# Transposing layer 1's queries in 128-column squares instead of per-head blocks of 96

## The chip, the cores and the metric

The kernel runs on one core of one Trainium2 chip. The metric is device time in microseconds. The kernel before has a median of 1709.44 us over three runs (1705.8 to 1714.31).

A core has five engines, each with its own in-order queue: TensorE (PE; its weight loads are shown apart as PEld), VectorE (DVE), ScalarE (ACT), GpSimd (POOL) and SyncE (SP), which here issues nearly all DMA transfers.

## The reference

Two transformer-like layers run over 1024 latent tokens and 256 context tokens of width 1024. Layer 0 is grouped-query attention, layer 1 multi-head latent attention with 16 heads. The part that matters here is how layer 1 makes its queries: a compressed projection of 384 columns is normalised, expanded to 16 heads x 96, normalised per head, and its last 32 of 96 entries are rotated. Scores are products of 96-long vectors.

```
def q_heads(q_a, n):
    q = (rms_norm(q_a, p["q_a_norm"]) @ p["w_q_b"]).reshape(B, n, MLA_HEADS, MLA_NOPE + MLA_ROPE)
    q = rms_norm(q, p["q_norm"])
    return jnp.split(q, [MLA_NOPE], axis=-1)
...
s = (jnp.einsum('bqhd,bkhd->bhqk', q_nope, k_nope)
     + jnp.einsum('bqhr,bkr->bhqk', q_rope, k_rope)).astype(jnp.float32) * ((MLA_NOPE + MLA_ROPE) ** -0.5)
p = jax.nn.softmax(s, axis=-1).astype(v.dtype)
return jnp.einsum('bhqk,bkhd->bqhd', p, v)
```

All of it is float32. The kernel keeps each matrix operand as two parts: a rounded high part and the remainder (low part). It forms a product from three matrix products, high x high, high x low and low x high (`mm3`, lines 93 to 95).

## The kernel before, in words

Layer 1 starts near 890 us. First keys and values are made, then (from about 990 us) the queries, then the attention over 16 heads (from about 1157 us), then the output projection (to the end).

The queries are made for 8 tiles of 128 tokens. For a tile, `q_compress` multiplies the modulated input by 384 columns and normalises (qan, line 1631). `q_latent` transposes that in three 128x128 blocks (line 1638) and splits it in a high part qah and a low part qal, which are also stored in memory (qad). `q_expand` multiplies them by 768 columns of the expansion weights, as two groups of 384 columns, and normalises and rotates; a group is four heads of 96 and lies as [128 tokens, 384 columns] in a tile t. `q_store` transposes each group into the layout that attention reads (columns on partitions, tokens along the row), splits it with `split` (ACT's copy th at line 86, DVE's subtraction tl at line 87) and stores both parts in device memory, in q1h and q1l, shaped [16 heads, 96, 1024 tokens].

The 768 columns are half of the 16 heads, so the 8 tiles are gone through twice. The first pass makes qah and qal; the second fetches them from qad. Each pass has 8 x 2 groups, so `q_store` handles 32 groups in all. Gate products (`gate_slice`, three matrix products per step, stored to sgd with gth) are mixed in, to give PE work in between. Also mixed in are weight loads (`load_weight`): a raw tile wraw is loaded, ACT rounds it to wa (line 157), and POOL or DVE makes the remainder wb (line 136).

Buffers around `q_store`: the transposes write into one of four PSUM tiles tp, which is free again when the subtraction tl has read it. The split writes into two staging tiles th and two tl, which are free when their store has landed.

Attention loads, for each head, the queries in halves of 512 tokens: QH (64 rows of q1h), QR (the 32 rotary rows), QL and QS (the same of q1l), with the keys KH and KL from k1h and k1l. First come maxima of the scores (mx, lines 393 and 403), then the scores (st, line 501), exponentials (p), and products with the values (av, line 555). KS is a key tile that is loaded when the last gate product has left its place (line 1529).

Outside a few parts that are written in a fixed order, the order of the instructions on each engine is set when the program is built, by a scheduler that goes by dependencies and by its own costs of instructions. A changed shape can therefore move neighbours, transfers on SP's queue among them.

Of the kernel before, what the change touches and what calls it, by code (L numbers as in the profile page):

```python
# [19 lines left out]
P = 128  # L20
# [11 lines left out]
def raw(ap):  # L32
    return ap.bitcast(F32)
# [3 lines left out]
def hybrid_kernel(ctx: ExitStack, tc: tile.TileContext, ins: dict, out: bass.AP):  # L37
    nc = tc.nc
    pe, act, dve, pool, sp = nc.tensor, nc.scalar, nc.vector, nc.gpsimd, nc.sync
# [16 lines left out]
    ident = const.tile([P, P], F32, name="ident")  # L56
# [13 lines left out]
    q1h = dram.tile([16, 96, NL], F32, name="q1h")  # L70
    q1l = dram.tile([16, 96, NL], F32, name="q1l")
# [13 lines left out]
    def split(hi, lo, src):  # L85
        act.copy(hi, src)  # L86
        dve.tensor_sub(lo, src, raw(hi))  # L87
# [975 lines left out]
    rows = {}  # L1063
# [530 lines left out]
    for p_ in range(8):  # L1594
        for par in range(2):
            h = 2 * p_ + par
# [6 lines left out]
    with ExitStack() as st:  # L1603
# [78 lines left out]
        def q_store(tt, c, held):  # L1682
            cs = slice(tt * P, (tt + 1) * P)
            for q4 in range(2):
                h0 = 8 * c + 4 * q4
                tp = ps_tp.tile([P, 512], F32, name="tp", tag="tp")
                for j in range(4):
                    pe.transpose(tp[:96, j * P:(j + 1) * P], held[q4][:, j * 96:(j + 1) * 96], ident)
                th = sg2.tile([P, 4, P], F32R, name="th", tag="th")
                tl = sg2.tile([P, 4, P], F32R, name="tl", tag="tl")  # L1690
                split(th[:96], tl[:96], tp[:96, :].rearrange("p (a n) -> p a n", n=P))
                sp.dma_start(q1h[h0:h0 + 4, :, cs].rearrange("a p n -> p a n"), raw(th[:96]))
                sp.dma_start(q1l[h0:h0 + 4, :, cs].rearrange("a p n -> p a n"), raw(tl[:96]))

        wqb = [load_weight(ins["l1_w_q_b"], 3, 0, 768,
                           slot=[wqp.tile([P, 2304], F32R, name=n) for n in ("wqa1", "wqb1")])]
# [6 lines left out]
        def store(c):  # L1703
            return lambda tt, held: q_store(tt, c, held)
# [95 lines left out]
```

## Time and profile before

| | |
|---|---|
| Median of three runs | 1709.44 us (1705.8 to 1714.31) |
| Profiled execution, own time | 1707.59 us |
| Its span | 1705.8 us |
| PE busy | 1667.9 us, 98% |
| DVE busy | 1046.6 us, 61% |
| POOL busy | 961.4 us, 56% |
| ACT busy | 645.1 us, 38% |
| Transposes of `q_store` | 128, first at 1030.1, last at 1134.8 us |
| Stores to q1h and to q1l | 32 and 32, 192 KB each |

The profile is of one execution. Times in its rows are microseconds from the start of the span; a row of the timeline gives start, duration, engine, line, operation, tiles (out<-in), shapes and count, and in brackets how long the engine had been idle and what ended that. A matrix product's recorded duration overlaps with its neighbours, so the cost of one in a run is the distance between starts. A row of waits says which instruction waited for which, for how long in total, how many times, and the longest. In rows with a bar the figures behind it are busy time in total, mean ns of one, and idle time before.

### The profile page before, as it was taken

To read this page: it belongs to the slowest core of one execution; us is meant where nothing else is said; L and a number is where in the kernel's file an instruction comes from. 1 tells how busy PE (TensorE), PEld (TensorE's weight loads), DVE (VectorE), ACT (ScalarE), POOL (GpSimd) and SP (SyncE) were. 2 spreads that over 40 slices of the span, in tenths; PEclk is the share of its full clock that TensorE was granted. 3 is DMA by queue.
4 is the path that set the end of the run, shared out by engine and by line. 5 is a ranking of instruction groups with operands and counts; after the bars stand their busy time and mean duration, and the time that the engine had idled before them with its cause. 6 is when DMAs were issued, how large, how long until landed. Compare 5 with 4: busy or idle time off the path is not lost. (4 is left out here: it accounts for less than half of the span.)

```text
span 1705.8 us, 27449 instructions
## 1 busy us (share of the span) xinstructions
PE 1667.9 (98%) x10244; PEld 1196.9 (70%) x10244; DVE 1046.6 (61%) x1807; ACT 645.1 (38%) x943; POOL 961.4 (56%) x646
## 2 busy tenths in 40 slices
PE   8999999999999999999989999999999999999998
PEld 5776778775555555557878898986767667667587
DVE  3765552357778777625675657754677777777231
ACT  4642221124445544432244533340434444344310
POOL 2763431218789988743245544350668787787511
PEclk9999999999999999999999999999999999999999
DMA  9557754521242422146433766766565655653452
GB/s 315 169 150 241 253 176 142 152 81 45 63 121 61 112 63 63 38 137 204 139 94 117 233 189 182 207 192 164 135 137 134 134 122 121 146 124 91 125 160 74
DMA packets 219821, 238.97 MB, mean 140 GB/s; under 512 B 23016, under 2 KB 159192, under 8 KB 219688
## 3 DMA queue, kind: packets, MB, share of 16 engines
q1 hardware_dynamic: 219264, 237.11, 49.5%
q8 instruction: 81, 1.33, 0.3%
q14 instruction: 52, 0.43, 0.1%
q10 hardware_dynamic: 424, 0.11, 0.0%
HBM read 163.37 MB, written 73.63 MB: 139 GB/s over the span
## 5 line engine op out<-in xcount | busy, mean ns | idle before, releaser
L395 DVE TENSOR_REDUCE m<-mx 128x1 f32<-128x512 f32 x512 | 336.2, 687 | 176.3 <-PE mx L393 170.5
L508 ACT ACTIVATE p<-st 128x1024 f32<-128x1024 f32 x328 | 336.0, 1027 | 169.8 <-PE st L501 134.8
L542 POOL TENSOR_TENSOR acp<-acp,p 128x1024 f32<-128x1024 f32 x128 | 305.8, 2389 | 7.8
L555 PE MATMUL av<-p,v 128*64 128x512 f32 x1312 | 289.9, 595 | 0.0
L555 PEld LDWEIGHTS av<-p,v 128*64 128x64 f32 x1312 | 90.9, 137 | 180.6 <-issue 177.9
L542 POOL TENSOR_TENSOR acp<-p 128x1024 f32<-128x1024 f32 x34 | 81.4, 2396 | 148.0 <-ACT p L508 147.9
L542 POOL TENSOR_TENSOR acp<-acp,acd 128x1024 f32<-128x1024 f32 x60 | 142.2, 2370 | 22.3 <-DVE acd L528 19.1
L528 DVE TENSOR_REDUCE acd<-p 128x512 f32<-128x1024 f32 x124 | 144.7, 1220 | 7.9 <-ACT p L508 7.8
L136 POOL TENSOR_TENSOR wb<-wraw,wa 128x512 fp32r<-128x512 f32 (+3 forms) x73 | 95.4, 1326 | 81.2 <-ACT wa L157 81.2
L93 PE MATMUL mm<-wa,hh 128*128 128x512 f32 (+2 forms) x336 | 127.4, 379 | 1.1 <-ACT hh L890 1.1
L501 PE MATMUL st<-QH,KH 64*128 64x512 f32 x320 | 122.2, 404 | 1.0 <-DVE gth L303 1.0
L95 PE MATMUL mm<-wa,hl 128*128 128x512 f32 (+2 forms) x336 | 121.5, 362 | 1.6 <-DVE hl L893 1.6
L94 PE MATMUL mm<-wb,hh 128*128 128x512 f32 (+2 forms) x336 | 121.2, 361 | 0.0
L501 PE MATMUL st<-QH,KL 64*128 64x512 f32 x320 | 119.0, 392 | 0.0
L501 PE MATMUL st<-QL,KH 64*128 64x512 f32 x320 | 118.3, 390 | 0.0
L576 ACT COPY os<-av 128x512 f32<-128x512 f32 x36 | 21.1, 587 | 255.9 <-PE av L555 205.9
L93 PE MATMUL y<-wa,oh 128*128 128x512 f32 (+1 forms) x296 | 114.1, 386 | 1.4 <-DVE yt L750 1.4
L95 PE MATMUL y<-wa,ol 128*128 128x512 f32 (+1 forms) x296 | 113.5, 384 | 0.0
L94 PE MATMUL y<-wb,oh 128*128 128x512 f32 (+1 forms) x296 | 113.5, 383 | 0.0
L404 DVE TENSOR_REDUCE m<-mx 128x2 f32<-128x512 f32 x144 | 95.4, 688 | 24.0 <-PE mx L403 18.9
L393 PE MATMUL mx<-KH,QH 64*128 64x512 f32 x256 | 102.7, 405 | 0.5 <-DVE m L404 0.3
L93 PE MATMUL mm<-hh,wa 128*128 128x512 f32 x256 | 102.0, 399 | 0.5 <-ACT th L86 0.5
(240 smaller groups left out, 4023.1 us busy)
## 6 DMA issues: line engine op xcount, KB each, us to landing
mraw<-in_l_w_mod SPq DMA_DIRECT2D x64, 256.0 KB
wraw<-in_l_w_in SPq DMA_DIRECT2D x28, 512.0 KB
KH<-k1h SPq DMA_DIRECT2D x32, 320.0 KB
KL<-k1l SPq DMA_DIRECT2D x32, 320.0 KB
rb<-rrow SPq DMA_DIRECT2D x72, 128.0 KB
mraw<-in_l_w_mod SPq DMA_DIRECT2D x16, 512.0 KB
sgd<-gth SPq DMA_DIRECT2D x32, 256.0 KB
wraw<-in_l_w_out SPq DMA_DIRECT2D x16, 512.0 KB
```

Of the source, the lines that this page charges most:

```text
L93: pe.matmul(ps, lhsT=lh(k), rhs=rh(k), start=first and i == 0, stop=False)
L94: pe.matmul(ps, lhsT=lh(k), rhs=rl(k), start=False, stop=False)
L95: pe.matmul(ps, lhsT=ll(k), rhs=rh(k), start=False, stop=last and i == len(ks) - 1)
L136: eng.tensor_sub(lo, a, b)
L393: pe.matmul(held["m"][:, cs], lhsT=q[:, t * P:(t + 1) * P], rhs=k[:, ks], start=j == 0, stop=j == len(pairs) - 1)
L395: dve.reduce_max(s["m"][:, i, n:n + 1], held["m"], axis=AX.X)
L404: dve.reduce_max(s["m"][:, 2 * i:2 * i + 2, 2 if u["kind"] == "lat" else 0], m.rearrange("p (a b) -> p a b", a=2), axis=AX.X)
L501: pe.matmul(ps[:, n * 512:(n + 1) * 512], lhsT=lh, rhs=rh, start=j == 0, stop=j == last)
L508: act.activation(p, ps, AF.Exp, scale=self.ops["scale"])
L528: dve.reduce_sum(t[:, ns], p2.rearrange("p a n -> p n a")[:, ns, :], axis=AX.X)
L542: pool.tensor_add(t, a, b)
L555: pe.matmul(s["av"][64 * n:64 * n + 64, :], lhsT=s["v"][:, kt, u["vc"]:u["vc"] + 64], rhs=p[:, n * 512:(n + 1) * 512], start=kt == kts[0], ...
```

## The change

`q_store` no longer transposes a group head by head. Before, four transposes took 96 columns each and wrote 96 partitions of the tile tp, four blocks of 128 tokens side by side: [96, 4 x 128]. Now three transposes take 128 columns each and write all 128 partitions: [128, 3 x 128]. The 384 columns of a group are the same, and so are the bytes. Row r of the three blocks put under each other is column r of the group, and because q1h is contiguous, (head, 96) can be read as 1536 rows, of which a group covers three blocks of 128. So the copy, the subtraction and the two stores now have the shape 128 x 3 x 128 where they had 96 x 4 x 128. What lies in memory is the same, and the loads of attention are not touched.

```
-                h0 = 8 * c + 4 * q4
+                rows = slice(3 * (2 * c + q4), 3 * (2 * c + q4) + 3)
                 tp = ps_tp.tile([P, 512], F32, name="tp", tag="tp")
-                for j in range(4):
-                    pe.transpose(tp[:96, j * P:(j + 1) * P], held[q4][:, j * 96:(j + 1) * 96], ident)
+                for j in range(3):
+                    pe.transpose(tp[:, j * P:(j + 1) * P], held[q4][:, j * P:(j + 1) * P], ident)
                 th = sg2.tile([P, 4, P], F32R, name="th", tag="th")
                 tl = sg2.tile([P, 4, P], F32R, name="tl", tag="tl")
-                split(th[:96], tl[:96], tp[:96, :].rearrange("p (a n) -> p a n", n=P))
-                sp.dma_start(q1h[h0:h0 + 4, :, cs].rearrange("a p n -> p a n"), raw(th[:96]))
-                sp.dma_start(q1l[h0:h0 + 4, :, cs].rearrange("a p n -> p a n"), raw(tl[:96]))
+                split(th[:, :3], tl[:, :3], tp[:, :384].rearrange("p (a n) -> p a n", n=P))
+                for dst, src in ((q1h, th), (q1l, tl)):
+                    sp.dma_start(dst.rearrange("h d n -> (h d) n").rearrange("(a p) n -> a p n", p=P)[rows, :, cs].rearrange("a p n -> p a n"),
+                                 raw(src[:, :3]))
```

The scheduler's order moves in three places that the prediction speaks of. On DVE, early in the query stage, this is the order before (t is a group's tile; wb the remainder of a weight piece, L136; tl the subtraction of `q_store`, L87):

```order
L1670 TENSOR_TENSOR t_10657<-mm,cwq 128x384
L1675 TENSOR_TENSOR qt_10659<-mm,swq 128x8x8 x2
L136 TENSOR_TENSOR wb<-wraw,wa 128x768
L1678 TENSOR_TENSOR t_10657<-t_10657,q_rs 128x384
L1665 TENSOR_REDUCE qss<-sq 128x4
L1670 TENSOR_TENSOR t_10682<-mm,cwq 128x384
L117 TENSOR_SCALAR q_ms<-qss 128x4
L1675 TENSOR_TENSOR qt_10684<-mm,swq 128x8x8 x2
L87 TENSOR_TENSOR tl<-tp,th 96x512
```

And now:

```order
L1670 TENSOR_TENSOR t_10655<-mm,cwq 128x384
L1675 TENSOR_TENSOR qt_10657<-mm,swq 128x8x8 x2
L1665 TENSOR_REDUCE qss<-sq 128x4
L1678 TENSOR_TENSOR t_10655<-t_10655,q_rs 128x384
L117 TENSOR_SCALAR q_ms<-qss 128x4
L1670 TENSOR_TENSOR t_10680<-mm,cwq 128x384
L1675 TENSOR_TENSOR qt_10682<-mm,swq 128x8x8 x2
L87 TENSOR_TENSOR tl<-tp,th 128x384
```

The weight piece wb no longer stands ahead of tl; it follows about 25 rows behind tl, and the reduction qss has moved up by one.

On SP, at the seam between the gate products and the first scores, this is the order before (QS from crow is a row of the maxima, sgd a gate store, v a load of values):

```order
L1541 DMA KH<-k1h 64x1280
L427 DMA QS<-crow 1x4x128 x2
L1529 DMA KS<-kr1h 32x1280
L304 DMA sgd_96<-gth 128x512
L1529 DMA KS<-kr1h 32x1280
L358 DMA v<-vd_94 128x10x128
L1542 DMA QH<-q1h 64x512
L1544 DMA QR<-q1h 32x512 x2
```

And now:

```order
L1541 DMA KH<-k1h 64x1280
L427 DMA QS<-crow 1x4x128 x2
L1542 DMA QH<-q1h 64x512
L1529 DMA KS<-kr1h 32x1280
L304 DMA sgd_96<-gth 128x512
L1529 DMA KS<-kr1h 32x1280
L358 DMA v<-vd_94 128x10x128
L1544 DMA QR<-q1h 32x512 x2
```

One load of QH has moved from behind the two KS loads to ahead of them.

On PE, at the end of the first pass, these are the transposes of two token tiles before (t is a group's tile, qah and qal the operands of the expansion):

```order
L1688 MATMUL tp<-ident,t_10739 96x128 x4
L1688 MATMUL tp<-ident,t_10764 96x128 x4
L1688 MATMUL tp<-ident,t_10811 96x128 x4
L1688 MATMUL tp<-ident,t_10836 96x128 x4
L93 MATMUL mm<-wa,qah 128x384
```

And now:

```order
L1688 MATMUL tp<-ident,t_10735 128x128 x3
L1688 MATMUL tp<-ident,t_10760 128x128 x3
L1688 MATMUL tp<-ident,t_10805 128x128 x3
L1688 MATMUL tp<-ident,t_10830 128x128 x3
L93 MATMUL mm<-wa,qah 128x384
```

Each group has three transposes where it had four, at the same place between the products.

## The prediction

> **What bounds the kernel now.** I read the page's busy times first, then the stages.
>
> ```profile
> span 1705.8 us, 27449 instructions
> PE 1667.9 (98%) x10244; PEld 1196.9 (70%) x10244; DVE 1046.6 (61%) x1807; ACT 645.1 (38%) x943; POOL 961.4 (56%) x646
> ```
>
> TensorE (PE) is busy for all but 37.9 of 1705.8 us, so what matters of an edit is what it takes out of PE's queue and what it does to PE's few waits. The busy table by stretch shows where the queries are made (1028 to 1146), the seam (1146 to 1210) and layer 1's attention behind it; columns are PE, weight loads, DVE, ACT, POOL, clock, DMA share, GB/s.
>
> ```profile
> 1028.00:1146.00 118.00, 114.56 (x628) 102.50 (x628) 85.10 (x209) 44.34 (x88) 54.69 (x65) 1.00 0.73 197
> 1146.00:1160.00 14.00, 13.79 (x58) 10.12 (x56) 3.31 (x6) 2.24 (x4) 2.54 (x2) 1.00 0.98 250
> 1160.00:1210.00 50.00, 47.10 (x245) 33.80 (x246) 26.03 (x41) 9.15 (x11) 8.68 (x5) 1.00 0.62 171
> 1210.00:1600.00 390.00, 389.95 (x2921) 261.20 (x2919) 279.31 (x403) 167.02 (x173) 294.90 (x142) 1.00 0.52 121
> ```
>
> In attention PE idles 0.05 of 390 us: nothing there can swallow or return a shift, so whatever the query stage saves or loses arrives at the end of the program in full. In the query stage PE idles 118.00 - 114.56 = 3.4 us. The waits of PE's instructions (and one of ACT's) between 990 and 1240 name the parts: us in total, times, longest.
>
> ```profile
> PE tp L1688 <- DVE tl L87: 2.8, 2, 1.4
> PE st L501 <- DMA KS<-kr1h: 1.6, 1, 1.6
> PE mm L93 <- ACT th L86: 0.5, 1, 0.5
> PE mx L393 <- DMA QH<-q1h: 0.2, 1, 0.2
> ACT th L86 <- DMA q1h<-th: 17.7, 8, 5.1
> ```
>
> Most of the loss in the stage is two waits of the very transposes that are edited: PE wants a PSUM buffer that DVE's subtraction (tl) has not yet left.
>
> **Term 1: 32 transposes fewer on PE.** There are 8 token tiles x 2 chunks x 2 groups = 32 groups; each goes from four transposes to three, 128 to 96 in all. The weights of a transpose are the query columns, its moving side is the 128-wide identity. What one costs in PE's queue is the spacing, not the recorded duration (they overlap), so I take runs of different length from the timeline, before and after a neighbour:
>
> ```profile
> 1063.64 1.04 PE L1688 MATMUL tp<-ident,t 128*96 128x128 f32 x8
> 1064.43 0.49 PE L93 MATMUL mm<-hh,wa 128*128 128x512 f32 x1
> 1070.02 1.91 PE L1688 MATMUL tp<-ident,t 128*96 128x128 f32 x16
> 912.91 1.03 PE L1506 MATMUL tp<-ident,kn 128*128 128x128 f32 x8
> 999.24 0.49 PE L1638 MATMUL tp<-ident,qan 128*128 128x128 f32 x3
> ```
>
> Eight more of the 96-wide kind lengthen a run by 1.91 - 1.04 = 0.87 us, 0.109 each. Of the 128-wide kind, five more cost 1.03 - 0.49 = 0.54 us, 0.108 each. The kind that is put in costs what the kind that goes costs, so a group saves one: 32 x 0.109 = 3.5 us, all of it on PE, which bounds. The weight loads do differ, which is the one thing that speaks against it:
>
> ```profile
> L1688 PEld LDWEIGHTS tp<-ident,t 128*96 128x96 f32 x128 | 14.2, 126 | 5.3 <-issue 3.8
> L1638 PEld LDWEIGHTS tp<-ident,qan 128*128 128x128 f32 x24 | 3.0, 141 | 1.4 <-issue 1.2
> L87 DVE TENSOR_TENSOR tl<-tp,th 96x512 fp32r<-96x512 f32 x32 | 21.3, 680 | 7.9 <-ACT th L86 5.2 <-DMA q1l<-tl 2.7
> L87 DVE TENSOR_TENSOR qal<-tp,qah 128x384 fp32r<-128x384 f32 x8 | 4.4, 547 | 0.0
> L86 ACT CAST th<-tp 96x512 fp32r<-96x512 f32 x32 | 17.8, 582 | 18.0 <-DMA q1h<-th 17.7 <-DVE gth L303 0.3
> L86 ACT CAST qah<-tp 128x384 fp32r<-128x384 f32 x8 | 3.8, 476 | 0.5 <-PE tp L1638 0.5
> ```
>
> A load of 128 columns takes 141 ns against 126, 15 ns more, but the spacing of 109 is below both and equal for both, so loads are overlapped and do not set it. By the load rows the bound from the other side would be 4 x 126 = 504 against 3 x 141 = 423, still a saving of 81 ns a group, 2.6 us. [...]
>
> **Term 2: shorter splits.** The last four rows price them: the new shape 128x384 exists already as the split of qan. DVE's subtraction goes from 680 to 547 ns, ACT's copy from 582 to 476: 32 x 0.133 = 4.3 us off DVE and 32 x 0.106 = 3.4 off ACT. Both are hidden work (85 and 44 us in that 118): they count only where PE waits for them, at two places.
>
> Wait A, at 1045, and wait B, at 1133.8:
>
> ```profile
> 1041.10 0.94 DVE L136 TENSOR_TENSOR wb<-wraw,wa 128x768 fp32r<-128x768 f32 x1
> 1044.13 0.68 DVE L87 TENSOR_TENSOR tl<-tp,th 96x512 fp32r<-96x512 f32 x1
> 1044.96 0.61 PE L1688 MATMUL tp<-ident,t 128*96 128x128 f32 x4 [1.43 <-DVE tl L87]
> ...
> 1071.69 0.43 PE L93 MATMUL mm<-wa,qah 128*128 128x384 f32 x1
> ...
> 1133.82 1.21 PE L1688 MATMUL tp<-ident,t 128*96 128x128 f32 x8 [1.41 <-DVE tl L87]
> ```
>
> As the order of DVE shown with the change has it, this weight conversion (0.94 us) now stands behind the tl that PE waits for at A. DVE waits for POOL and ACT in between, so not all of it is won: from 0 up to the whole wait of 1.43; I take 0.6, between, by the tl's own 0.13 and half of the 0.94. The conversion is late then by some microseconds, but its weights are first read by the second chunk's products at 1071.69, over 25 us on. Wait B (1.41) has its DVE rows in the same order in both programs; in the 16 us before it DVE has two shorter subtractions ahead (0.13 to 0.27 earlier) and PE four fewer transposes (0.44 earlier), so the wait stays within 0.3 of what it is: 0, with -0.4 to +0.4.
>
> **Term 3: the stores.** Each of 64 stores keeps 384 runs of 512 B, 192 KB, but takes them from 128 partitions x 3 rather than 96 x 4. They sit on a chain that ends at the first query load of attention:
>
> ```profile
> 1133.54 4.46 DMA q1h<-th
> 1140.11 3.75 DMA q1h<-th
> 1145.28 4.87 DMA q1l<-tl
> 1152.95 4.35 DMA QH<-q1h
> 1157.44 0.59 PE mx L393 x2
> ```
>
> PE's first maximum waited 0.18 us for that load (the 0.2 above): there is no cover. Because PE comes earlier by term 1, the chain has to come earlier too. It does: it hangs on products and splits of the same stage, and after wait B it loses three copies and one subtraction (3 x 0.106 + 0.133 = 0.45) where PE loses two transposes (0.22). Against it stands SyncE's issue:
>
> ```profile
> L1643 SPq DMA_DIRECT2D qad<-qal x8: 359/360/377, 1000.2 to 1047.2; - x8
> L1693 SPq DMA_DIRECT2D q1l<-tl x32: 304/315/819, 1034.1 to 1145.3; - x32
> ```
>
> At their shortest 359 ns for the 128-partition form, 304 for the 96: 55 ns more for each, three on this chain, 0.17 us. Net 0. How the transfers' own time changes no row shows. Bounds: as fast as now, or a fifth either way of 4.46 + 3.75 + 4.87 = 13.1 us, 2.6 us. Faster can win only the 0.2; slower costs all 2.6. I take 0, because bytes and runs are equal.
>
> [...]
>
> **Term 4: loads moved at the seam.** One query load (QH) now stands ahead of the two KS loads on SyncE. These queue behind it, and PE waits for them (1.6 above). SyncE was idle just there:
>
> ```profile
> SPq L1529 <- PE mm L95: 2.3, 1, 2.3
> 1198.25 0.74 SPq L1542 DMA_DIRECT2D QH<-q1h  x1
> ```
>
> KS cannot be issued before the last gate product, and SyncE waited 2.3 us for it; a 0.74 us issue fits in. So 0, or up to +0.6 if its 128 KB is still moving when the second KS load starts.
>
> **Sum.** -3.5 - 0.6 + 0 + 0 = -4.1 us. Ends: -3.5 - 1.4 - 0.4 - 0.2 = -5.5 at best, and with PE saving nothing 0.4 + 2.6 + 0.6 = +3.6 at worst. The span goes from 1705.8 to 1701.7; the profiled execution's own time was 1707.59 and becomes 1703.5. It lies 1.85 under the median of 1709.44, so the median becomes about 1705.3; I say 1705.
>
> **Rivals.**
> *Loads set the pace, by columns.* A group loads 384 columns in both programs (4 x 96, 3 x 128); if columns set PE's pace, only wait A is won: 1709.4 - 0.6 = 1708.8. For it: PEld is busy 102.5 of the 118 us. Against it: the spacings. 10%.
>
> *Stores shorten and the waits go.* ACT waited 17.7 us for stores to leave its two staging buffers; if these land earlier, splits run earlier, and PE's 2.8, 0.5 and 0.2 all go: 3.5 + 3.5 = 7.0 us, 1702.4. For it: all three waits are of this stage. Against it: wait B hangs on DVE's order and not on a store. 17%.
>
> *The last stores land late (slower).* At 1133 to 1150, with the transfers at 0.98 of their capacity at the end of it, the three stores of the chain run one after the other, each holding a buffer that the next copy needs, and PE's first maximum has no cover. Should a store of 128 partitions take longer, all goes into PE: from 4.1 of 13.1 us (31% longer) on the kernel is slower than before; at 60% it is 7.8 - 4.1 = +3.7, 1713.1. For it: no cover, a longer issue. Against it: equal bytes and runs. 9%.
>
> *It does not do what it says:* the order of PE has 96 transposes in groups of three where 128 stood, so this is 1%, 1709.
>
> The forecast keeps 63%.
>
> **How the numbers follow.** The runs of before lie 8.5 us apart, 0.5% of the time, which is about what a measurement can tell from no change. The range takes in the second rival, the first and most of the third, with some of that scatter: 1699 to 1713. Below 1700.9 (faster by 0.5%) lie some of the second rival and the tail of the forecast: 13%. Above 1718 only an extreme of the third: 5%. Within: 82%.
>
> **What would show it.** Right: 96 transposes at 1688 with spacing 0.109; PE busy about 3.5 us less between 1028 and 1146; tl at about 547 ns; wait A at half; the first maximum waiting under 0.5 us; attention's 390 us stretch unchanged, only earlier. Wrong: transposes spaced at 0.14 or more; a wait of microseconds of the first maxima for QH, or of KS at the seam; a difference that starts before 1028, where the programs are alike.

## The result and the profile after

| | before | changed |
|---|---|---|
| Median of 22 runs each | 1708.99 us (1704.83 to 1715.51) | 1704.95 us (1701.49 to 1709.98) |
| Ratio, 95% interval | | 0.9975 (0.9966 to 0.9984) |
| Span of the profiled execution | 1705.8 us | 1701.4 us |
| First transpose of the query stage to the first maximum | 1030.09 to 1156.76: 126.67 us | 1027.87 to 1151.54: 123.67 us |

The kernel became 4.3 us faster, between 2.7 and 5.8. That is 0.25%: within the 0.5% that the prediction calls no change, and yet, with 22 runs of each, clear of zero. (One execution of the changed kernel among the experiments ran at a mean granted clock of 0.752, in 2044.51 us; no figure below includes it.)

The head of the page of the changed kernel:

```profile
span 1701.4 us, 27386 instructions
PE 1663.7 (98%) x10212; PEld 1195.3 (70%) x10212; DVE 1042.7 (61%) x1807; ACT 641.6 (38%) x943; POOL 961.3 (57%) x646
```

PE is busy 4.2 us less, DVE 3.9 less and ACT 3.5 less. The stages, in the windows that the prediction used (columns PE, weight loads, DVE, ACT, POOL, clock, DMA share, GB/s):

```profile
1028.00:1146.00 118.00, 114.18 (x607) 101.60 (x606) 80.01 (x206) 42.58 (x90) 56.99 (x66) 1.00 0.73 211
1160.00:1210.00 50.00, 47.05 (x264) 34.54 (x264) 27.12 (x44) 11.20 (x13) 13.14 (x7) 0.97 0.52 139
1210.00:1600.00 390.00, 389.95 (x2906) 259.37 (x2905) 275.42 (x397) 164.42 (x172) 294.00 (x142) 1.00 0.53 122
```

Attention again idles 0.05 of its 390 us, so what the query stage wins is kept to the end. But in the query stage PE now idles 3.8 us where it idled 3.4, although wait A has shrunk. The waits of PE (and one of ACT) name what grew:

```profile
PE tp L1688 <- DVE tl L87: 3.4, 4, 1.5
PE st L501 <- DMA KS<-kr1h: 1.7, 1, 1.7
PE mm L93 <- DVE qt L1675: 0.4, 1, 0.4
ACT th L86 <- DMA q1h<-th: 15.2, 8, 5.0
```

The transposes wait four times for DVE's subtraction where they waited twice; the wait for QH is gone from the list. PE's timeline shows which four:

```profile
1027.87 0.82 PE L1688 MATMUL tp<-ident,t 128*128 128x128 f32 x6
1041.68 0.52 PE L1688 MATMUL tp<-ident,t 128*128 128x128 f32 x3 [0.92 <-DVE tl L87]
1066.07 1.47 PE L1688 MATMUL tp<-ident,t 128*128 128x128 f32 x12
1068.46 0.52 PE L1688 MATMUL tp<-ident,t 128*128 128x128 f32 x3 [0.21 <-DVE tl L87]
1070.12 0.52 PE L1688 MATMUL tp<-ident,t 128*128 128x128 f32 x3 [0.79 <-DVE tl L87]
1079.85 0.47 PE L93 MATMUL mm<-hh,wa 128*128 128x512 f32 x1 [0.44 <-DVE qt L1675]
1128.81 0.98 PE L1688 MATMUL tp<-ident,t 128*128 128x128 f32 x6 [1.46 <-DVE tl L87]
1151.54 0.50 PE L393 MATMUL mx<-KH,QH 64*128 64x512 f32 x2
```

Twelve transposes last 1.47 us and six 0.82, so one costs (1.47 - 0.82) / 6 = 0.108 us. Wait A (now at 1041.68) is 0.92 where it was 1.43. Wait B (1128.81) is 1.46 where it was 1.41. Two waits near 1070 are new, and the first maxima start without one. The sizes of the shorter splits and of the stores' issue, from the tiles' own rows (min/median/max in ns):

```profile
L86 ACT CAST th<-tp x32: 468/479/502, 1028.8 to 1137.8; 128x384 fp32r<-128x384 f32 x32
L87 DVE TENSOR_TENSOR tl<-tp,th x32: 540/551/559, 1031.2 to 1138.6; 128x384 fp32r<-128x384 f32 x32
L1693 SPq DMA_DIRECT2D q1l<-tl x32: 359/360/977, 1031.8 to 1139.2; - x32
```

The first row of the timeline also shows that this execution was 2.2 us ahead of the kernel before's by 1028, where the two programs are alike. So the two profiled spans, 4.4 us apart, are not a clean measure of the change; a length between two marks on PE is the better one. What the 2.2 us are is told at the end.

Up to the first maximum, which is called the stage from here on, the changed kernel is 3.0 us shorter. But the first maxima go quicker too. The kernel before, then the changed one (its first maxima are the last row above):

```profile
1156.76 0.50 PE L393 MATMUL mx<-KH,QH 64*128 64x512 f32 x1
1157.44 0.47 PE L393 MATMUL mx<-KH,QH 64*128 64x512 f32 x1 [0.18 <-DMA QH<-q1h]
1196.94 0.50 PE L501 MATMUL st<-QH,KH 64*128 64x512 f32 x1 [0.98 <-DVE gth L303]
```

```profile
1190.99 0.50 PE L501 MATMUL st<-QH,KH 64*128 64x512 f32 x1 [0.98 <-DVE gth L303]
```

Before, the second maximum started 0.68 us behind the first, with a wait for QH in between; now the two start together. From the first maximum to the first product of the scores (L501) PE takes 39.45 us where it took 40.18, with the same number of products in between. So from the first transpose to that product it is 163.12 us where it was 166.85: 3.7 us less.

### The profile page after: what moved, and what is told of

Its sections match the earlier page's. It is cut to its first block, busy times and chain, and to the rows that moved or that the text cites. A ratio compares the mean times of both kernels' runs of the same rounds, so it can differ in the third digit from the quotient of the medians.

```text
span 1701.4 us, 27386 instructions
## 1 busy us (share of the span) xinstructions
PE 1663.7 (98%) x10212; PEld 1195.3 (70%) x10212; DVE 1042.7 (61%) x1807; ACT 641.6 (38%) x943; POOL 961.3 (57%) x646
## 5 line engine op out<-in xcount | busy, mean ns | idle before, releaser
L542 POOL TENSOR_TENSOR acp<-acp,acd 128x1024 f32<-128x1024 f32 x60 | 141.9, 2365 | 22.3 <-DVE acd L528 19.2
L136 POOL TENSOR_TENSOR wb<-wraw,wa 128x512 fp32r<-128x512 f32 (+3 forms) x73 | 96.1, 1335 | 78.7 <-ACT wa L157 78.6
L501 PE MATMUL st<-QH,KH 64*128 64x512 f32 x320 | 122.9, 407 | 1.0 <-DVE gth L303 1.0
L501 PE MATMUL st<-QH,KL 64*128 64x512 f32 x320 | 119.6, 395 | 0.0
L501 PE MATMUL st<-QL,KH 64*128 64x512 f32 x320 | 118.9, 392 | 0.0
```

The costliest lines, as they stand in the source:

```text
L136: eng.tensor_sub(lo, a, b)
L501: pe.matmul(ps[:, n * 512:(n + 1) * 512], lhsT=lh, rhs=rh, start=j == 0, stop=j == last)
L542: pool.tensor_add(t, a, b)
```

## The experiments

The theory: PE is the bound, a transpose costs 0.109 us whether it is 96 or 128 columns wide, so 32 fewer win 3.5 us; wait A adds half a microsecond; stores and splits are hidden. The rivals: weight loads set the pace by their columns; the stores' new shape sets the time, either way; the stage's waits hang on staging buffers. In the diffs, "before" and "changed" say which kernel was edited.

### The fourth transpose put back

Changed kernel, with one more 128-wide transpose per group into the unused quarter of the PSUM tile; nobody reads it. (With it the scheduler puts the weight conversion back ahead of tl, as in the kernel before.)

```
                 for j in range(3):
                     pe.transpose(tp[:, j * P:(j + 1) * P], held[q4][:, j * P:(j + 1) * P], ident)
+                pe.transpose(tp[:, 384:512], held[q4][:, 0:P], ident)
```

> The changed kernel with a fourth 128-wide transpose put back in each group; it writes the fourth block of tp, which nothing reads. Splits and stores stay in the new shape. The order on DVE goes back to having the weight piece wb ahead of the tl of wait A. Theory (the saving is PE's, one transpose per group, plus wait A): both gains go, 1709.0 - 0 to 0.5, ratio to before 0.9995 to 1.0005, and PE's busy time is back to about 1667. Rival (the saving comes from shorter splits or from better spread stores): it stays at about 0.9975.

Measured: 1707.77 us, ratio 0.9993 (0.998 to 1.0006). The centre is just under the range that was expected, and the lower end of the interval touches the change's (0.9966 to 0.9984), so the times alone do not quite part the two kernels. The profile does: the stage takes 127.07 us, 3.4 more than in the changed kernel, and PE is busy for 123.3 us of it (123.2 before the change, 119.9 with it). Splits and stores have their new shape in this kernel, so they did not bring the gain; the number of transposes did, with the order at wait A (1.28 us here), which came back with it.

### The stores alone

As above, and the copy and subtraction go over four blocks again, so that of the change only the stores' 128 x 3 shape (and the width of the transposes) is left.

```
-                split(th[:, :3], tl[:, :3], tp[:, :384].rearrange("p (a n) -> p a n", n=P))
+                split(th, tl, tp.rearrange("p (a n) -> p a n", n=P))
```

> As the kernel with four transposes, and the splits take all four blocks (128 x 512) again, so that ACT and DVE work as long as before; of the changed kernel only the stores of 128 x 3 runs are left. Theory (stores change nothing, since bytes and runs are equal and PE does not wait for them): ratio 0.999 to 1.001, copies at 582 and subtractions at 680 ns. Rival (stores of 128 partitions are quicker, buffers come free earlier, PE's waits go): 0.996 to 0.998. Other rival (stores slower): 1.001 and more.

Measured: 1709.71 us, ratio 0.9993 (0.998 to 1.0006), the same ratio as with short splits. The split's length and the stores' shape are not seen in the time. In the profile the stage takes 127.70 us, 0.63 more than with short splits: wait A is 1.42 us where it was 1.28, and the second wait for tl is 1.7 where it was 0.9. In one profile of each, then, the shorter splits win something at PE's waits that these times are too coarse to show.

### Four transposes more, narrow and wide

The disputed price by itself: the kernel before, with four extra transposes per group (128 in all) ahead of its own, whose results its own overwrite. In one kernel the extra ones take 96 columns as weights, in the other 128.

```
+                for j in range(4):
+                    pe.transpose(tp[:96, j * P:(j + 1) * P], held[q4][:, j * 96:(j + 1) * 96], ident)
```

```
+                for j in (0, 1, 2, 0):
+                    pe.transpose(tp[:, j * P:(j + 1) * P], held[q4][:, j * P:(j + 1) * P], ident)
```

> The kernel before with four extra transposes of 96 columns per group, ahead of the four real ones, which overwrite them: 128 extra. Theory (109 ns of PE each, all on the path): 128 x 0.109 = 14.0 us, ratio 1.0082, spacing 0.109 in the timeline. If PE had slack in the stage: less, down to 1.006.

> The same with four extra transposes of 128 columns per group. Theory (the 128-wide moving side sets the pace): the same 14.0 us, ratio 1.0082, and within 1 us of the kernel with narrow ones. Rival (weight loads set the pace, by columns): a third more than the narrow ones, 18.6 us, ratio 1.0109. By the recorded load durations, 141 to 126 ns: 15.6 us, 1.0092.

Measured: narrow 1718.42 us, ratio 1.006 (1.0038 to 1.0083); wide 1719.37 us, ratio 1.0055 (1.004 to 1.0069). The intervals lie over each other, and the rows say why. First the narrow kernel's timeline, then the wide one's (L1688 and L1690 are the two loops of four):

```profile
1026.82 0.60 PE L1688 MATMUL tp<-ident,t 128*96 128x128 f32 x4
1027.25 0.60 PE L1690 MATMUL tp<-ident,t 128*96 128x128 f32 x4
```

```profile
1028.90 0.60 PE L1688 MATMUL tp<-ident,t 128*128 128x128 f32 x4
1029.34 0.60 PE L1690 MATMUL tp<-ident,t 128*96 128x128 f32 x4
```

Four narrow ones take 0.43 us to the next start, four wide ones 0.44. Over the stage the wide kernel is longer by 137.98 - 137.54 = 0.44 us, 3 ns a transpose; a pace set by columns would have made it a third of 14 us longer, 4.7. That rival has fallen. That the moving side sets the pace is not shown by this: it is 128 wide in every row here.

The price itself was expected at 14.0 us and the stage grew by 137.54 - 126.67 = 10.9. PE's busy time in it did grow by about that (136.74 against 123.23, 13.5 us), but its idle time fell by 2.6 (0.80 against 3.44), since both waits for tl are no longer in the list of waits: 13.5 - 2.6 = 10.9. Of the 13.5 us of work that was added to PE, 2.6 came out of its waits.

### A third pair of staging buffers

The new waits near 1070 follow a subtraction that itself waited 1.1 us for the store that held its staging tile:

```profile
1069.42 0.56 DVE L87 TENSOR_TENSOR tl<-tp,th 128x384 fp32r<-128x384 f32 x1 [1.11 <-DMA q1l<-tl]
```

Three blocks instead of four per tile leave room for a third pair.

```
-        sg2 = st.enter_context(tc.tile_pool(name="stg1b", bufs=2, **right))
+        sg2 = st.enter_context(tc.tile_pool(name="stg1b", bufs=3, **right))
-                th = sg2.tile([P, 4, P], F32R, name="th", tag="th")
-                tl = sg2.tile([P, 4, P], F32R, name="tl", tag="tl")
+                th = sg2.tile([P, 3, P], F32R, name="th", tag="th")
+                tl = sg2.tile([P, 3, P], F32R, name="tl", tag="tl")
```

> The changed kernel with three staging tiles for th and for tl instead of two, each cut to the three blocks that are used. Theory: the changed kernel's new waits of PE at 1068 to 1070 (0.21 and 0.79) hang on a tl that waited for a store to leave its staging tile, so they go, and ACT's 15.2 us of waits for stores of q1h nearly go; the wait at 1128.8 (1.46), which hangs on DVE's order, stays. So 1.0 us below the changed kernel: ratio to before 0.9969. Rival (it is the stores that hold all of PE's waits for tl): all 3.4 us go, 0.9955. Other rival (waits are passed on to the next buffer): 0.9975.

Measured: 1702.16 us (1699.55 to 1708.01), ratio 0.9958 (0.9944 to 0.9971): faster than the kernel before, and under the changed kernel too, though those two intervals overlap. PE's wait for the transposes and ACT's for the stores:

```profile
PE tp L1688 <- DVE tl L87: 2.7, 2, 1.8
ACT th L86 <- DMA q1h<-th: 5.1, 3, 4.0
```

The two new waits are gone; A (0.90) and B (1.78) stay. ACT's 15.2 us for stores became 5.1, of which PE felt only a little: the stage takes 122.15 us, 1.5 less than the changed kernel's. The ratio is near the rival's 0.9955, but the rival's mechanism, all waits for tl gone, did not come.

### The conversion ahead of wait B, moved to POOL

Wait B hangs on DVE's weight conversions (L136). Here POOL makes all of that weight's remainders.

```
-        wg1 = load_weight(w_in1, KT, 1184, 512)
+        wg1 = load_weight(w_in1, KT, 1184, 512, 0)
```

> The changed kernel with the remainders wb of the second gate weights (eight pieces of 128 x 512) all made by POOL, where DVE made half. Theory (the wait at 1128.8 hangs on DVE, which has a conversion of 4.06 us and another of 0.68 ahead of the tl): that wait of 1.46 goes, 0.9967, unless POOL, which also makes q_rs of the same groups, becomes what PE waits for: then 0.9975 or more, up to 0.999.

Measured: 1708.93 us, ratio 0.9997 (0.9984 to 1.001), a little above the rival's range: the whole gain of the change is lost. PE's timeline:

```profile
1129.49 0.99 PE L1688 MATMUL tp<-ident,t 128*128 128x128 f32 x6 [1.80 <-POOL wb L136]
1153.65 0.47 PE L393 MATMUL mx<-KH,QH 64*128 64x512 f32 x1 [0.95 <-DMA QH<-q1h]
```

The wait is there, larger, and POOL is named for it. The name alone says little, since the changed kernel's second profile (below) names POOL for the same wait at 1.46 us. What shows the rival's mechanism is DVE's row ahead of the subtraction:

```profile
1126.65 1.62 DVE L1678 TENSOR_TENSOR t<-t,q_rs 128x384 f32<-128x384 f32 x1 [6.15 <-POOL t L1677]
```

DVE waits 6.15 us for POOL's part of t, which stands behind six conversions (7.86 us together, 1.3 each); in the changed kernel it waited 1.37 us there. Still, that is not where the time is lost. The stage takes 1152.21 - 1029.10 = 123.11 us, 0.56 less than the changed kernel's, because PE idles less at the turn between the passes (told below). The loss lies behind it: the second maximum waits 0.95 us for QH, and the granted clock is 0.82 and 0.84 in the two windows of 10 us from 1150 to 1170, which is 3.4 us lost. So most of the loss in this profile is the clock's; that QH is late because of wait B is not shown by itself. Both edits together:

> Both of the last two edits. Theory: of PE's 3.4 us of waits for tl only the one at 1041 (0.9) stays, 0.9961. Rival (POOL is the new bound): 0.997 to 0.999.

Measured: 1704.01 us, ratio 0.9971 (0.9957 to 0.9985), with a wait of 2.08 us put down to POOL's conversion. The stage takes 122.57 us, 0.4 more than with the third buffer alone; the times do not part these two, since their intervals overlap.

### Every store issued twice

Changed kernel, each store to q1h and q1l issued a second time with the same data. This asks what late stores would cost, which was the slower rival's ground.

```
                     sp.dma_start(dst.rearrange(...)[rows, :, cs].rearrange("a p n -> p a n"), raw(src[:, :3]))
+                    sp.dma_start(dst.rearrange(...)[rows, :, cs].rearrange("a p n -> p a n"), raw(src[:, :3]))
```

> The changed kernel with every store to q1h and q1l made twice (same bytes to the same place), to price stores that land late. Theory of the prediction (no cover between the last stores and PE's first maximum): the three stores of the chain take about twice their 13 us, PE waits for QH by 5 us or more, and for tl in the stage besides: ratio to before 1.001 to 1.008, that is 6 to 18 us above the changed kernel. Rival (there is cover after all, since in the changed kernel the first maximum does not wait): at most 2 us above the changed kernel, 0.9975 to 0.9987.

Measured: 1730.21 us, ratio 1.0127 (1.011 to 1.0145), 25 us over the changed kernel and above the range expected. PE's waits:

```profile
PE tp L1688 <- DVE tl L87: 9.2, 5, 5.3
PE mx L393 <- DMA QH<-q1h: 4.9, 1, 4.9
PE st L501 <- DMA KS<-kr1h: 4.2, 1, 4.2
PE mm L95 <- DMA qal<-qad: 4.0, 3, 1.7
```

The rival's mechanism is real: late stores hold the buffers, the splits and the first load of attention, as it said, and more that it left out: the fetch of qal, and KS behind it on the same queue. The rows sum to 22.3 us where the changed kernel had 3.4 + 1.7 for the same lines, 17 us more; by an estimate from the mean clock over the span, 0.991 in these four runs against 0.9955 in the changed kernel's, the clock adds some 8. What did not happen is its condition: in the change the stores were not late.

### The changed kernel again, and the third buffer on the same chip

> The changed kernel, nothing edited, on another chip, beside the two kernels below. Theory (what was read from its first profile belongs to the program): ratio to before 0.9975 (0.9966 to 0.9984); from the first transpose of the query stage to the first maximum 123.7 us again, within 0.5; the two waits for tl near 1068 and 1070 are there again (1.0 us together, within 0.3), wait A near 0.9 and wait B near 1.5. The short falls of the granted clock may stand at other places, since they differed between executions of programs that are alike there. Rival (the first profile was one draw of the traffic): the two waits near 1070 are gone or the stage is over 1 us longer or shorter.

> The changed kernel with a third pair of staging buffers, as before, now on the same chip as the changed kernel itself. Theory (the third buffer takes away the two waits near 1070 and what follows from them): 1.0 to 1.5 us under the changed kernel, a ratio to before of 0.9967 to 0.9969 where the changed kernel has 0.9975. Rival (the first measurement's 2.8 us under the changed kernel holds): 0.9958. Third way (it was noise between chips): the same as the changed kernel, 0.9975.

Measured on one chip: changed kernel 1706.96 us over twelve runs, ratio 0.9984 (0.9968 to 0.9999); with the third buffer 1704.47 us, ratio 0.9968 (0.9958 to 0.9979). The changed kernel's gain is there again, and the third buffer's, 2.5 us on top, nearer the rival's 2.8 than the 1.0 to 1.5 expected, though the two intervals overlap; its stage takes 1151.76 - 1029.53 = 122.23 us. The changed kernel's second profile is from one more run:

> The changed kernel once more, for a second profile at full clock. Theory: 123.7 us from the first transpose to the first maximum, within 0.5 apart from falls of the granted clock inside that stretch; two waits for tl near 1068 and 1070, 1.0 us together within 0.3; wait A near 0.9, wait B near 1.5. Rival (the first profile was one draw of the traffic): those two waits are gone, or the stage is over 1 us longer or shorter at full clock.

Its timeline:

```profile
1031.22 0.82 PE L1688 MATMUL tp<-ident,t 128*128 128x128 f32 x6
1083.20 0.47 PE L93 MATMUL mm<-hh,wa 128*128 128x512 f32 x1 [1.31 <-DVE qt L1675]
1132.16 0.98 PE L1688 MATMUL tp<-ident,t 128*128 128x128 f32 x6 [1.46 <-POOL wb L136]
1154.88 0.58 PE L393 MATMUL mx<-KH,QH 64*128 64x512 f32 x2
1194.65 0.49 PE L501 MATMUL st<-QH,KH 64*128 64x512 f32 x1 [0.98 <-DVE gth L303]
```

The stage takes 1154.88 - 1031.22 = 123.66 us, the first profile's to 0.01; to the first product of the scores it is 163.43 us, 3.4 under the kernel before. Wait A is 0.87 us and wait B 1.46. But the two waits near 1070 are gone, as the rival said, and a wait of 1.31 us for qt at 1083.20 stands in their place. So neither answer was whole: which instruction waits differs between these two executions, the sum does not. The 39 us around this place, the turn from the first pass to the second, give the sum. The kernel before, the changed kernel, its second profile, and the third buffer (37 us of it; it has the same runs of transposes in them):

```profile
1054.00:1093.00 39.00, 38.40 (x217) 34.47 (x216) 27.72 (x76) 13.04 (x27) 14.51 (x20) 1.00 0.79 214
```

```profile
1050.00:1089.00 39.00, 37.56 (x205) 33.49 (x204) 27.52 (x77) 12.06 (x26) 14.78 (x20) 1.00 0.75 216
```

```profile
1054.00:1093.00 39.00, 37.56 (x207) 33.64 (x206) 27.39 (x75) 12.06 (x27) 14.65 (x20) 1.00 0.79 222
```

```profile
1051.00:1088.00 37.00, 36.98 (x203) 33.25 (x202) 26.66 (x76) 11.75 (x26) 14.77 (x20) 1.00 0.77 218
```

PE idles 0.60 us there before, 1.44 in both profiles of the changed kernel, and 0.02 with the third buffer. The change loses 0.84 us of its gain at this place.

Why it does is open. It is not simply that a quicker PE runs into its buffers: in windows of the same length around the turn PE idles 1.55 us in the kernel with the fourth transpose put back and 1.01 us in the one with the stores alone, and both have as many transposes as the kernel before. With the conversion moved to POOL it is 0.55 us. So with two staging pairs it varies from program to program.

### The third buffer without the change

The kernel before, four blocks of 96, with the third pair of staging buffers alone. To make room, a small tile of statistics gives up its spare copies.

```
-        sg2 = st.enter_context(tc.tile_pool(name="stg1b", bufs=2, **right))
+        sg2 = st.enter_context(tc.tile_pool(name="stg1b", bufs=3, **right))
-            ss = small.tile([P, 1], F32, name="qass", tag="qass")
+            ss = small.tile([P, 1], F32, name="qass", tag="qass", bufs=1)
```

> The kernel before, with its four transposes of 96, and a third pair of staging buffers alone (one small statistics tile gives up its spare copies to make room; its scheduler order moves a little). Theory (before the change no store held PE: its two waits for tl hang on the order of DVE): ACT's wait for q1h falls from 17.7 us to some 5, PE's waits for tl stay at 2 to 3.5 us, and the time is the kernel's before within 0.5 us, ratio 0.9997 to 1.0003. Rival (waits for staging buffers reached PE in the kernel before as well): PE's waits for tl fall under 1.5 us and the time by 1.5 to 3 us, ratio 0.9982 to 0.9991.

Measured: 1709.99 us, ratio 0.9996 (0.9983 to 1.001); stage 1160.68 - 1034.03 = 126.65 us, before 126.67.

```profile
PE tp L1688 <- DVE tl L87: 3.1, 2, 1.7
ACT th L86 <- DMA q1h<-th: 7.5, 3, 4.8
```

```profile
1200.10 0.50 PE L501 MATMUL st<-QH,KH 64*128 64x512 f32 x1 [0.98 <-DVE gth L303]
```

ACT's 17.7 us of waiting for stores falls to 7.5, and up to the first maximum nothing is won, as the theory has it. Behind it something is: the first maxima no longer wait for QH, and from the first transpose to the first product of the scores it is 1200.10 - 1034.03 = 166.07 us where it was 166.85. So in the kernel before the two staging pairs cost PE 0.8 us, at a place where the row of waits names only 0.2; the times are too coarse to show it. In the changed kernel they cost 1.6 us to the same mark (161.57 us with the third pair, 163.12 without), and there it is the turn between the passes, where PE idles 0.02 us with the third pair. Whether the wait for the store itself or the order of DVE and PE that the scheduler makes with three pairs (subtractions and gate products stand at other places there) does it, these runs do not tell apart.

## Why the prediction was right

The forecast was 1705.0 us with a range of 1699 to 1713; the median is 1704.95. By the profiles, where the change can be seen alone, the sum is 3.0 us up to the first maximum and 3.7 (3.4 in the second profile) up to the first product of the scores, and not 4.1. All of these lie within the interval of the times (2.7 to 5.8), so the closeness of the medians is in part luck. Step by step:

- **Term 1, 32 transposes fewer, -3.5 us: right.** The spacing is 0.108; the fourth transpose put back takes the gain away; 96 and 128 columns differ by 3 ns. The step from equal spacings to "loads are overlapped" was sound, and with it the first rival has fallen. The load rows have 141 ns against 126, 12% more for a third more columns, and neither sets the pace here.
- **Term 2, the shorter splits: sizes right, one place missed.** The split takes 551 and 479 ns where 547 and 476 were taken from another tile's rows. Wait A fell by 0.5 us (0.6 taken), wait B stayed (1.46 against 1.41). The step that failed is "they count only where PE waits for them, at two places". There is a third place: at the turn between the passes the changed kernel idles 0.84 us more. The list of waits of the kernel before showed 0.5 us of it (a product that waited for th), and I read past it, since it was not a wait of the edited instruction. So -3.5 - 0.5 + 0.84 + 0.05 = -3.1, and the stage shows -3.0. What part of the change makes the turn worse is not shown.
- **Term 3, the stores, 0: no loss, as said, but a gain that was put too low.** The issue takes 359 ns, as the other store's rows said. From the issue of the first q1h store of the chain to that of KH it was 1133.54 to 1150.24, 16.7 us, and is now 1128.66 to 1143.65, 15.0. The load of QH was issued 5.2 us ahead of the first maximum (3.8 before), and the wait for it is gone. So the chain became quicker by more than PE did. The step "Faster can win only the 0.2" took the idle time in the row for the whole price; the waiting maximum stood 0.68 us behind the first, and from the first maximum to the first product of the scores PE won 0.7 us (0.4 in the second profile). The stores' shape alone does not do it: with the fourth transpose put back, and the same stores and short splits, the chain is 1134.33 to 1150.58, 16.25 us, and the wait for QH is there. That is 0.45 us under the 16.70 of before, but the chain holds products and splits too, and no run here measures a store alone. The fifth either way by which the prediction bounded the stores was the author's estimate, and no run shows it.
- **Term 4, QH ahead of KS, 0: right.** The wait for KS is 1.7 us, before 1.6.
- **The rivals.** "Stores shorten and the waits go" did not happen: ACT's wait for stores is 15.2 us against 17.7, and wait B is where it was; of its three waits only the one for QH went. In the kernel before a third buffer left both waits for tl as well. "The last stores land late" has its mechanism (the stores issued twice) but not its condition.
- **What would have shown it wrong:** of the three signs, one came, a difference ahead of 1028. It is not the change, as the last section shows, and it flatters the profiled span by 2.2 us.

## What to carry to other kernels

On an engine that is the bound, count the instructions of a kind by their spacing in runs of different length, not by their duration or by the columns they load; a short test with extra instructions of both widths settles it (here 0.108 and 0.109 us apart at 128 and 96 columns, with loads of 141 and 126 ns). A saving on that engine must then be walked through every place where it already waits a little, and not only the waits of the edited lines: there a part of it can turn into waiting (0.84 us here, at the turn between the passes), and the buffers have to be looked at again (here a third staging pair is worth 0.8 us without the change and 1.6 us with it, at different places). And when a difference is a quarter of a per cent, compare the length between two marks on the bound engine, in two profiles, rather than two spans, and set the second mark behind the last wait that the edit can move: the first maximum was too early by 0.7 us here.

## What the runs showed of the hardware that was not expected

A wait of PE cost more than itself in some of the profiles: the granted clock dropped behind it, to 0.50 in the rows below. At the seam, PE waits about 1.0 us for gth and 1.5 to 1.8 for KS in the kernel before, in the changed one and with the third buffer. In windows of 2 us (the column before the last two is the clock), this is the third buffer's first profile, then its second:

```profile
1194.00:1196.00 2.00, 2.00 (x21) 1.94 (x19) 1.42 (x3) 1.34 (x2) 0.00 (x0) 1.00 1.14 330
1196.00:1198.00 2.00, 2.00 (x20) 1.96 (x18) 1.76 (x3) 1.40 (x2) 1.14 (x1) 1.00 1.17 310
```

```profile
1192.00:1194.00 2.00, 0.85 (x8) 0.38 (x4) 1.10 (x2) 0.00 (x0) 0.26 (x1) 0.88 0.84 229
1194.00:1196.00 2.00, 1.39 (x6) 1.25 (x8) 0.13 (x1) 0.59 (x1) 0.00 (x0) 0.50 1.10 300
1196.00:1198.00 2.00, 2.00 (x12) 1.71 (x10) 1.02 (x2) 0.43 (x1) 0.00 (x0) 0.50 1.18 310
1198.00:1200.00 2.00, 2.00 (x12) 1.67 (x12) 0.93 (x2) 1.02 (x1) 0.44 (x1) 0.50 1.09 358
```

It is the same program and nearly the same waits (1.45 and 1.76 us for KS). In the one PE goes on at full clock, 20 products in 2 us; in the other at half, 12; summed over the windows from 1192 to 1202 (clock 0.88, three times 0.50, 0.91) it loses 3.4 us. Their spans are 1699.2 and 1702.8 us, 3.6 apart. Other dips are half as long. In windows of 10 us:

```profile
980.00:990.00 10.00, 7.39 (x36) 7.20 (x37) 5.21 (x7) 4.48 (x7) 6.88 (x4) 0.83 0.92 259
```

```profile
980.00:990.00 10.00, 8.45 (x51) 8.25 (x52) 5.69 (x7) 4.64 (x7) 5.85 (x3) 1.00 0.93 267
1190.00:1200.00 10.00, 7.36 (x49) 6.24 (x50) 4.94 (x8) 2.63 (x4) 3.17 (x3) 0.83 0.91 246
```

The first is the kernel before, the other two rows the changed kernel. A clock of 0.83 over 10 us is 1.7 us lost. The kernel before had this at 980, behind waits of 1.96 and 0.80 us for kn; the changed kernel had nearly the same waits (1.89 and 0.79) and no dip, which is 1.7 of the 2.2 us that it was ahead by 1028. It paid the same 1.7 at 1190, behind KS, where the kernel before paid nothing. In all thirteen profiles other than the one at 0.752 there is a dip near 880, at a wait that is 4.99 to 5.71 us long in the five whose rows there were read; in the kernel before the clock is down to 0.50 in the window from 878 to 880, while PE still waits (until 880.62). Near 980 there is a dip in eight of the thirteen, at 1190 to 1220 in seven.

By the windows of 10 us, each dip at these three places costs about 1.7 us (one window at 0.83, say) or about twice that (0.89 and 0.77 side by side near 880 in the kernel before, 3.4 us). Why nearly the same wait is charged in one execution and not in the next, no run here shows, nor how long PE must idle for it. At the seam the idle time was not in one piece: between 1190 and 1194 the changed kernel was busy 1.69 of 4 us, with waits of 0.98 and 1.66 us, 2.6 together, and the clock fell to 0.50 from 1196 to 1198; the kernel before had waits of 0.98 and 1.60 us there, and its clock stayed at 1.00.
